# Two output tiles and a raw weight buffer trade pools in a hybrid RWKV/pool/expert layer

## The chip, the cores and the metric

The kernel runs on one core of a Trainium2 chip. The metric is device microseconds of one execution. A profiled execution leaves a trace of every instruction on the five engines (PE for matmuls, DVE, ACT, POOL, and SP, which here only issues transfers) and of every transfer; times in it count from the first instruction.

## The reference, cut to what matters

One layer is computed for 1056 positions (1024 of a prompt, 32 of samples). Behind the mixing part stands the expert part, with 16384 single-neuron experts of which each position uses 8 x 16:

```python
q = (xb @ wq).reshape(PEER_BLOCK, PEER_HEADS, 2, PEER_DK_HALF)
s1 = jnp.einsum('thc,nc->thn', q[:, :, 0], sub_keys[0])
s2 = jnp.einsum('thc,nc->thn', q[:, :, 1], sub_keys[1])
v1, i1 = lax.top_k(s1, PEER_TOPK)
v2, i2 = lax.top_k(s2, PEER_TOPK)
...
ue = jnp.take(u_tab, expert, axis=0)
act = jax.nn.gelu(jnp.einsum('thkd,td->thk', ue, xb).astype(jnp.float32), approximate=False) * gate
ve = jnp.take(v_tab, expert, axis=0)
return jnp.einsum('thk,thkd->td', act.astype(xb.dtype), ve)
```

A gated embedding and a last norm follow.

## The kernel before, in words

The positions are worked in four groups (`GROUPS`). For each group `phase_c` makes the output projection and the norm, then the queries from 16 blocks of `wq`, and writes scores to DRAM (`sc_d`). `top` and `select` then pick experts on DVE. For the first 672 positions (`ND`) the experts are computed densely: the gates are spread into a full table `g_d` in DRAM, by one-hot tiles `ab` that DVE builds (L905 to L907), matmuls over them (L913), a copy into a staging tile `gst` on ACT (L914) and a write of 2 MB per 32 positions (L916). These matmuls are called gate matmuls below. The other 384 positions gather their experts one by one on POOL (L1229).

The dense part takes all 128 expert blocks of `u` (u blocks, `ublock`) and then of `v` (v blocks, `vblock`). Each block is a raw weight tile of 512 KB loaded by SP (L1094), split into two parts for an exact product by `esplit` (`ehi` by ACT at L1096, `elo` by DVE at L1098, or by POOL through `PTT`, L127), and 48 matmuls (L1120) of 128 by 336 over the stored input `XH`, `XL`, or over gated activations `wh`, `wl`. A u block ends in a Gelu on ACT (L1126) that writes an activation tile. The first eight u blocks (`NPRE`, numbered 0 to 7 here) write into the tiles `OT0` to `OT7`, which later hold the sums of the v blocks; the others write into `wt`. `ugate` multiplies an activation tile with its gates, loaded back from `g_d` into `gq` (L1174, L1177), and splits it into `wh` and `wl` (L1181). The first v block needs the gated activations of u blocks 0 to 7.

The part around the change is step 4 of the loop over groups. There the gate table of the third group's last 128 positions is still being made (`t_stream`), `phase_c` runs for the fourth group, and `upre` traces u blocks 0 to 7 between its pieces. The last six of the fourth group's `wq` blocks go through `esplit` as well (`C3E`), the others load ready-made halves `whi` and `wlo` of 256 KB each (L644, L645, three buffers each).

Memory is given out by pools, and a tile that reuses room waits until its last user is done. Pool `dr` is opened before step 4 in room that is free by then. Pool `late` is opened inside step 4 after `gstack.close()`, in the room of pool `gp`, which holds `gst`, `ab` and the one-hot sources. `gp` stays in use until the last gate matmul. In the kernel before, `dr` holds `XH`, `XL`, three raw buffers `eraw`, two each of `ehi` and `elo`, and `OT0` to `OT5`; `late` holds `OT6`, `OT7` and three `wt`.

Buffers of one name are handed out in the order in which the program traces their users. A scheduler then writes each engine's instructions in a fixed order, from priorities in that order and its own estimate of when room and inputs are there. On the chip each engine and the SP queue go through their list in that order.

Of the kernel before, what the change touches and what calls it, by code (L numbers as in the profile page):

```python
# [10 lines left out]
F32 = mybir.dt.float32  # L11
# [9 lines left out]
KB = D // 128  # L21
# [21 lines left out]
ND = GB - GA  # L43
# [20 lines left out]
def body(ctx, tc, io):  # L64
# [557 lines left out]
    def wblock(gi, b):  # L622
        if b >= C3E and gi == NG - 1:
            hi, lo = esplit(io["wq"][b - KB], PTT)
            return [(t[0], t[1]) for t in zip(*[(x[:, :HK], x[:, HK:]) for x in (hi, lo)])]
        out = []
        for i in range(1 if b < KB else 2):
            ks = slice(i * HK, (i + 1) * HK)
            hi = ws.tile([128, HK, 128], F32R, name="whi", bufs=3)
            lo = ws.tile([128, HK, 128], F32R, name="wlo", bufs=3)  # L630
            if gi == 0:
                if b < 4:
                    raw = tk.tile([128, HK, 128], F32, name="wraw", tag="oh", bufs=2)
                else:
                    if b % 4 == 0 and i == 0:
                        wraws[0] = gp.tile([128, EB, TC], F32, name="gst", bufs=2)
                    raw = v3(wraws[0][:, 16 * (b % 4 if b < KB else 2 * (b % 4) + i):][:, :16].rearrange("p a b -> p (a b)"), 128)
                nc.sync.dma_start(raw, (io["w_out"][b] if b < KB else io["wq"][b - KB])[:, ks, :])
                ACT(hi, raw, AF.Copy)
                TT(lo, raw, hi.bitcast(F32), op=ALU.subtract)  # L640
                nc.sync.dma_start(wc_d[b, :, 0, ks, :], hi.bitcast(F32))
                nc.sync.dma_start(wc_d[b, :, 1, ks, :], lo.bitcast(F32))
            else:
                nc.sync.dma_start(hi.bitcast(F32), wc_d[b, :, 0, ks, :])  # L644
                nc.sync.dma_start(lo.bitcast(F32), wc_d[b, :, 1, ks, :])  # L645
            out.append((hi, lo))
        return out
# [438 lines left out]
    DP = ((0, NH), (NH, NH))  # L1086
    U = {}

    def PD():
        return dps.tile([128, 2, 512], F32, name="pd")  # L1090

    def esplit(src, sub=TT):
        raw = dr.tile([128, KB, 128], F32, name="eraw", bufs=3)
        nc.sync.dma_start(raw, src)  # L1094
        hi = dr.tile([128, KB, 128], F32R, name="ehi", bufs=2)
        ACT(hi, raw, AF.Copy)  # L1096
        lo = dr.tile([128, KB, 128], F32R, name="elo", bufs=2)
        sub(lo, raw, hi.bitcast(F32), op=ALU.subtract)  # L1098
        return hi, lo

    OT = {}

    def otile(db):
        if db not in OT:
            OT[db] = (dr if db < KB - 2 else late).tile([128, ND], F32, name=f"OT{db}")
        return OT[db]

    def wt_tile():
# [13 lines left out]
    def ublock(b, sub=TT):  # L1122
        ps = PD()
        emm(ps, esplit(io["uT"][b], sub), xs, DP)
        U[b] = otile(b) if b < NPRE else wt_tile()
        ACT(halves(U[b]), ps[:, :, :NH], AF.Gelu)  # L1126
# [7 lines left out]
    for step in range(1, NG + 1):  # L1134
# [8 lines left out]
        if step == NG:  # L1143
# [3 lines left out]
            late = ctx.enter_context(tc.tile_pool(name="late", bufs=1, side="right", reuse_waits="tile"))  # L1147
# [3 lines left out]
        if step == NG - 1:  # L1151
            nc.sync.dma_start(io["wkv_p"], S[-1])
            pbx.close()
            dr = ctx.enter_context(tc.tile_pool(name="dr", bufs=1, side="right", reuse_waits="tile"))
# [29 lines left out]
    def vblock(g, db):  # L1184
        w = esplit(io["vP"][g, db])
        ps = PD()
        emm(ps, w, [Ws[b] for b in range(g * VG, (g + 1) * VG)], DP)
        if g:
            TT(halves(OT[db]), ps[:, :, :NH], halves(OT[db]), op=ALU.add)  # L1189
        else:  # L1190
            ACT(halves(OT[db]), ps[:, :, :NH], AF.Copy)
        if g == EB // VG // 2:
            ht = wt_tile()
            nc.sync.dma_start(ht, hT_d[:, db, GA:GB])
            TT(OT[db], OT[db], ht, op=ALU.add)
# [88 lines left out]
    class Tail:  # L1284
# [10 lines left out]
        def gate(self, db, w, pl, mul):  # L1295
            ps = PD()
            emm(ps, w, self.xs, self.parts)
            sg = self.tmp()
            for a, (s, k) in enumerate(self.parts):
                TT(sg[:, s:s + k], ps[:, a, :k], self.r[:, s:s + k], op=ALU.mult)  # L1300
            ACT(sg, sg, AF.Sigmoid)
            if db == KB - 1:
                ACT(small()[:, 0:1], eps_t, AF.Sqrt)
            mul(sg, sg, pl[:, self.o:self.o + self.n], op=ALU.mult)
            l = TT(self.src[db], self.src[db], sg, op=ALU.add).ins
            if db < KB - 1:
                square(self.acc, self.src, db, self.tmp())
            else:
                self.more = [self.tmp()]
                ACT(self.more[0], self.src[db], AF.Square)  # L1310
            return l
# [137 lines left out]
def program(arrays, extra=()):  # L1449
    nc = bacc.Bacc("TRN2", target_bir_lowering=False, num_devices=1)  # L1450
    io = {k: nc.dram_tensor(k, v.shape, mybir.dt.from_np(v.dtype), kind="ExternalInput").ap()
          for k, v in arrays.items()}
    for k, s in list(OUTS.items()) + list(extra):
        io[k] = nc.dram_tensor(k, s, F32, kind="ExternalOutput").ap()
    with tile.TileContext(nc, schedule_with_timeline_sim=True) as tc, ExitStack() as ctx:
        body(ctx, tc, io)
    return nc
# [15 lines left out]
```

## Time and profile before

| | |
|---|---|
| median of 3 runs | 3257.71 us (3257.33 to 3266.85) |
| the profiled execution | 3253.73 us, its span 3252.0 us |
| PE busy | 3096.8 us, 95% of the span |
| DVE, POOL, ACT busy | 80%, 43%, 34% |
| mean granted TensorE clock | 0.975 of full speed |

A row of an instruction group gives engine, line, operation and tiles, then count and durations. A row of a chain or a timeline gives the start in us, the length in us, and what ran. A row of windows gives, for a stretch of time, the busy us of each engine with the number of its instructions, then the granted clock (1.00 is full), the share of the transfer engines that was busy, and GB/s.

### The profile page before, as it was taken

What the parts mean: (1) busy time and instruction counts of PE and PEld (TensorE: products, weight loads), DVE (VectorE), ACT (ScalarE), POOL (GpSimd) and SP (SyncE); (2) the same over time, 40 slices, a digit from 0 to 9 for tenths busy, and PEclk for the clock granted to TensorE, in tenths of its full rate; (3) what the DMA queues carried; (4) which work ended last, traced back from release to release, by engine and by line L of the source; (5) the groups of instructions that cost most, each with busy time, mean ns of one, the idle gap of its engine ahead of it and who ended that gap; (6) DMA issues with size and microseconds to landing.
All of it is one profiled execution on the core that took longest, in us unless ns stands there. A gap on an engine that the chain in (4) does not pass through costs nothing.

```text
span 3252.0 us, 66214 instructions
## 1 busy us (share of the span) xinstructions
PE 3096.8 (95%) x26807; PEld 2978.2 (92%) x26807; DVE 2586.6 (80%) x5094; ACT 1111.1 (34%) x1710; POOL 1389.1 (43%) x1069
## 2 busy tenths in 40 slices
PE   8998899989989688999999999999999999999998
PEld 7887788878878588999999999999999999999997
DVE  6776345479898995988889888888888888888955
ACT  6442323435645553322122222222212212222343
POOL 5211400020020241156666666656566666666632
PEclk9999899989999799999999999999999999999998
DMA  3326467968877868389999999999999999999834
GB/s 119 113 96 147 131 167 225 301 175 255 248 225 235 275 213 277 115 308 332 331 342 349 317 348 345 321 335 355 326 326 347 332 331 338 342 326 343 316 98 139
DMA packets 436419, 858.93 MB, mean 264 GB/s; under 512 B 109841, under 2 KB 230929, under 8 KB 431633
## 3 DMA queue, kind: packets, MB, share of 16 engines
q1 hardware_dynamic: 324848, 448.82, 42.8%
q0 software_dynamic: 111264, 405.88, 34.5%
q8 instruction: 210, 3.44, 0.4%
q14 instruction: 97, 0.79, 0.1%
HBM read 733.99 MB, written 120.60 MB: 263 GB/s over the span
## 4 chain that ended last, share of the span: by engine, by line
PE 81%; DVE 8%; DMA 7%; ACT 2%; issue 1%; POOL 0%; SPq 0%; DVEq 0%; ACTq 0%; POOLq 0%
PE pd L1120 59%; PE ps L470 6%; PE ps L219 4%; PE ps L655 3%; PE ps L657 2%; PE ps L656 2%; DMA wlo<-wc_d 2%; PE ps L913 1%; DMA whi<-wc_d 1%; PE ps L302 1%; PE ps L743 1%; DVE ab L905 1%; PE ps L1027 1%; DMA scq<-sc_d 1%; DMA hx_d<-x 1%
## 5 line engine op out<-in xcount | busy, mean ns | idle before, releaser
L1229 POOL DMA_INDIRECT row<-u,idx x384 | 548.0, 1427 | 311.1 <-DVE row L1237 126.5
L1096 ACT ACTIVATE ehi<-eraw 128x1024 fp32r<-128x1024 f32 x274 | 290.7, 1061 | 1130.9 <-PE pd L1120 1025.4
L1229 POOL DMA_INDIRECT row<-v,idx x384 | 534.6, 1392 | 316.6 <-DVE po L1246 144.0
L1120 PE MATMUL pd<-XL,ehi 128*128 128x336 f32 x2176 | 515.4, 317 | 0.0
L1120 PE MATMUL pd<-XH,elo 128*128 128x336 f32 x2176 | 514.9, 317 | 0.3 <-DVE elo L1098 0.2
L1120 PE MATMUL pd<-XH,ehi 128*128 128x336 f32 x2176 | 512.2, 316 | 2.1 <-DVE tt L1300 2.1
L1120 PE MATMUL pd<-wl,ehi 128*128 128x336 f32 (+1 forms) x2112 | 502.3, 316 | 1.5 <-DVE wl L1181 1.4
L1120 PE MATMUL pd<-wh,elo 128*128 128x336 f32 (+1 forms) x2112 | 503.3, 317 | 0.4 <-DVE elo L1098 0.4
L1120 PE MATMUL pd<-wh,ehi 128*128 128x336 f32 (+1 forms) x2112 | 503.0, 317 | 0.0
L1246 DVE SCALAR_TENSOR_TENSOR po<-row,act,po 128x1024 f32<-128x1024 f32 x381 | 488.5, 1282 | 6.7
L1237 DVE SCALAR_TENSOR_TENSOR row<-row,xt 128x1024 f32<-128x1024 f32 x384 | 455.5, 1220 | 7.1 <-DMA xt<-xt_d 3.5
L1098 DVE TENSOR_TENSOR elo<-eraw,ehi 128x1024 fp32r<-128x1024 f32 x260 | 319.7, 1229 | 75.8 <-ACT ehi L1096 75.2
L1120 PEld LDWEIGHTS pd<-XH,ehi 128*128 128x128 f32 x2176 | 372.5, 189 | 2.6 <-DVE tt L1300 2.5
L1120 PEld LDWEIGHTS pd<-XH,elo 128*128 128x128 f32 x2176 | 373.6, 188 | 0.9 <-DVE elo L1098 0.5
L1120 PEld LDWEIGHTS pd<-XL,ehi 128*128 128x128 f32 x2176 | 371.6, 188 | 0.0
L1120 PEld LDWEIGHTS pd<-wl,ehi 128*128 128x128 f32 x2112 | 361.9, 188 | 2.4 <-DVE wl L1181 2.3
L1120 PEld LDWEIGHTS pd<-wh,elo 128*128 128x128 f32 x2112 | 361.1, 188 | 0.8 <-DVE elo L1098 0.6
L1120 PEld LDWEIGHTS pd<-wh,ehi 128*128 128x128 f32 x2112 | 361.7, 188 | 0.1
L655 PE MATMUL ps<-hi,whi 128*128 128x256 f32 (+1 forms) x592 | 186.8, 317 | 27.6 <-DMA whi<-wc_d 17.2
L1189 DVE TENSOR_TENSOR OT<-pd,OT 128x672 f32<-128x672 f32 x120 | 102.9, 858 | 137.8 <-PE pd L1120 137.2
L914 ACT ACTIVATE gst<-ps 128x512 f32<-128x512 f32 x168 | 170.4, 1105 | 71.7 <-PE ps L913 64.5
L657 PE MATMUL ps<-hi,wlo 128*128 128x256 f32 (+1 forms) x592 | 183.2, 310 | 6.6 <-DMA wlo<-wc_d 6.1
(441 smaller groups left out, 5023.9 us busy)
## 6 DMA issues: line engine op xcount, KB each, us to landing
eraw<-uT SPq DMA_DIRECT2D x128, 512.0 KB, 6.4
eraw<-vP SPq DMA_DIRECT2D x128, 512.0 KB, 6.6
g_d<-gst SPq DMA_DIRECT2D x21, 2048.0 KB, 9.6
gq<-g_d SPq DMA_DIRECT2D x32, 1344.0 KB, 10.2
whi<-wc_d SPq DMA_DIRECT2D x108, 256.0 KB, 4.5
wlo<-wc_d SPq DMA_DIRECT2D x108, 256.0 KB, 4.9
fdc<-fd SPq DMA_DIRECT2D x16, 896.0 KB, 8.4
wc_d<-whi SPq DMA_DIRECT2D x40, 256.0 KB, 4.3
```

The lines of the kernel that those rows point to most:

```text
L219: mm(ps[:, :XW], s[:, k, :], x[:, k, a:b], start=first, stop=last)
L470: mm(o[hs], l[hs], r[hs], start=start, stop=stop)
L655: mm(ps[:, :n], whi[:, kk, :], xhi[:, k, :n], start=k == 0, stop=False)
L657: l = mm(ps[:, :n], wlo[:, kk, :], xhi[:, k, :n], start=False, stop=k == K - 1)
L914: ACT(st[:, :, t2 + q:t2 + q + 4].rearrange("p e t -> p t e"), v3(ps, 128), AF.Copy, scale=1.0 / GS)
L1096: ACT(hi, raw, AF.Copy)
L1098: sub(lo, raw, hi.bitcast(F32), op=ALU.subtract)
L1120: mm(ps[:, a, :n], w_[:, k, :], x_[:, s:s + n], start=first, stop=last)
L1189: TT(halves(OT[db]), ps[:, :, :NH], halves(OT[db]), op=ALU.add)
L1229: nc.gpsimd.indirect_dma_start(out=r[:m], out_offset=None, in_=io[tab], in_offset=bass.IndirectOffsetOnAxis(ap=idx[:m, hh, k:k + 1], axis=0))
L1237: STT(r[:m], r[:m], 1.0, xt[:m], op0=ALU.mult, op1=ALU.mult, accum_out=pre[:m, k:k + 1])
L1246: STT(po[:m], r[:m], act[:m, k:k + 1], po[:m], op0=ALU.mult, op1=ALU.add)
```

## The change

`OT6` and `OT7` move from `late` to `dr`. In exchange the raw buffers `eraw` of `dr` go from three to two, and every third call of `esplit` takes its raw tile from a new single buffer in `late`. `late` is already set when `esplit` is first called, so calls 3, 6, 9 and so on use it. In the order of tracing these are u block 2, u block 5, one `wq` block, u block 7, and then every third block to the end.

```diff
+    late, raws = None, [0]
...
     def esplit(src, sub=TT):
-        raw = dr.tile([128, KB, 128], F32, name="eraw", bufs=3)
+        raws[0] += 1
+        third = raws[0] % 3 == 0 and late is not None
+        raw = late.tile([128, KB, 128], F32, name="eraw3") if third else dr.tile([128, KB, 128], F32, name="eraw", bufs=2)
         nc.sync.dma_start(raw, src)
...
     def otile(db):
         if db not in OT:
-            OT[db] = (dr if db < KB - 2 else late).tile([128, ND], F32, name=f"OT{db}")
+            OT[db] = dr.tile([128, ND], F32, name=f"OT{db}")
         return OT[db]
```

No instruction is added or removed; the lists are rewritten. Behind the change all line numbers from the dense part on are four higher (L1094 becomes L1098, L1120 becomes L1124).

The SP queue before, where the raw tiles of the first u blocks are loaded (`eraw_15119`, `15242`, `15365`, `15576`, `15752` are those of u blocks 0 to 4; `whi`, `wlo` are weight halves for `phase_c`):

```order
L686 DMA y_15076<-y_d_64 128x4x256
L1094 DMA eraw_15119<-uT 128x1024
L1094 DMA eraw_15242<-uT 128x1024
L1094 DMA eraw_15365<-uT 128x1024
L762 DMA scq_16419<-sc_d_68 128x512
L916 DMA g_d_72<-gst_14090 128x32x128
L1094 DMA eraw_15576<-uT 128x1024
L644 DMA whi_15219<-wc_d_70 128x512
L645 DMA wlo_15220<-wc_d_70 128x512
L1094 DMA eraw_15752<-uT 128x1024
```

The SP queue now, at the end of the fourth group's weight loads; `gst_14971` is the staging tile of the last gate matmuls:

```order
L645 DMA wlo_16023<-wc_d_70 128x512
L762 DMA scq_18243<-sc_d_68 128x512
L916 DMA g_d_72<-gst_14971 128x32x128
L1098 DMA eraw3_15365<-uT 128x1024
L1178 DMA gq_16649<-g_d_72 128x2688
L1178 DMA gq_16671<-g_d_72 128x2688
L1098 DMA eraw3_15911<-uT 128x1024
L1098 DMA eraw_16052<-wq 128x1024
L1098 DMA eraw_16085<-uT 128x1024
```

The raw load of u block 2 (`15365`) moved from the third place of the loads to behind the last write of the gate table; those of u blocks 5 and 6 (`15911`, `16085`) and of the first `wq` block (`16052`) follow it. The loads of u blocks 0, 1, 3 and 4 stand early in both lists.

PE before, at the start of u block 2 (`pd_15364`), between a projection block of `phase_c` (`ps_15324`) and gate matmuls (`ab_14335`):

```order
L656 MATMUL ps_15324<-lo_15088,whi_15320 128x256
L657 MATMUL ps_15324<-hi_15087,wlo_15321 128x256
L1120 MATMUL pd_15364<-XH_14394,ehi_15367 128x336 x2
L1120 MATMUL pd_15364<-XL_14395,ehi_15367 128x336 x2
L1120 MATMUL pd_15364<-XH_14394,elo_15369 128x336 x2
L1120 MATMUL pd_15364<-XH_14394,ehi_15367 128x336 x2
L1120 MATMUL pd_15364<-XL_14395,ehi_15367 128x336 x2
L1120 MATMUL pd_15364<-XH_14394,elo_15369 128x336 x2
L1120 MATMUL pd_15364<-XH_14394,ehi_15367 128x336 x2
L913 LDWEIGHTS ab_14335
L913 MATMUL ps_14339<-ab_14335 128x128
```

PE now, at the start of the same u block; `ps_16026` is the last `wq` block with ready-made halves, and the last gate matmuls stand 22 matmuls ahead of `pd_15364`:

```order
L655 MATMUL ps_16026<-hi_15448,whi_16022 128x256
L656 MATMUL ps_16026<-lo_15449,whi_16022 128x256
L657 MATMUL ps_16026<-hi_15448,wlo_16023 128x256
L1124 MATMUL pd_15364<-XH_14394,ehi_15367 128x336 x2
L1124 MATMUL pd_15364<-XL_14395,ehi_15367 128x336 x2
L1124 MATMUL pd_15575<-XH_14394,ehi_15578 128x336 x2
L1124 MATMUL pd_15575<-XL_14395,ehi_15578 128x336 x2
L1124 MATMUL pd_15364<-XH_14394,elo_15369 128x336 x2
L1124 MATMUL pd_15364<-XH_14394,ehi_15367 128x336 x2
```

U block 2 and with it u blocks 3 to 6 (`pd_15575`, `15751`, `15910`, `16084`), which before stood in pieces between the gate matmuls and the projections, now stand in one row behind the last gate matmul. U blocks 0 and 1 stay where they were. Behind the six split `wq` blocks and u blocks 7 and 8, from the first v block on, the lists of all engines run as before, but for the places of a few matmuls at the very end.

## The prediction

> **What bounds the kernel now.** I read the page first, then a table of windows through step 4 and one of the dense stretch, then the chain of waits, the SP queue and the waits of DVE around the last gate matmul.
>
> ```profile
> PE 3096.8 (95%) x26807; PEld 2978.2 (92%) x26807; DVE 2586.6 (80%) x5094; ACT 1111.1 (34%) x1710; POOL 1389.1 (43%) x1069
> ```
> ```profile
> 2400.00:3100.00 700.00, 700.00 (x4563) 699.97 (x4562) 610.27 (x728) 170.99 (x204) 440.47 (x312) 1.00 0.92 330
> ```
> ```profile
> L1126 ACT ACTIVATE OT<-pd x8: 712/734/748, 1124.1 to 1288.4; 128x672 f32<-128x672 f32 x8
> ...
> L1120 PE MATMUL pd<-wh,ehi x52: 311/316/322, 1303.4 to 1329.5; 128*128 128x336 f32 x52
> ```
>
> In the dense stretch PE never stops: 700 us in 700, so 0.1534 us per matmul and 7.36 us per block of 48. Nothing can be won or lost there by buffers. The first v block starts at 1303.4. What counts is when that happens; all behind it follows in the same order. The eight u blocks that must precede it end between 1124.1 and 1288.4, inside step 4:
>
> ```profile
> 1080.00:1100.00 20.00, 8.54 (x70) 6.75 (x68) 20.00 (x95) 8.23 (x11) 3.16 (x8) 0.50 1.07 377
> 1100.00:1120.00 20.00, 15.33 (x114) 14.00 (x112) 20.00 (x76) 11.59 (x16) 10.18 (x6) 0.77 0.88 298
> 1120.00:1140.00 20.00, 17.89 (x152) 16.73 (x150) 20.00 (x66) 13.23 (x20) 5.95 (x5) 1.00 0.65 175
> 1140.00:1160.00 20.00, 19.59 (x153) 19.12 (x153) 19.36 (x80) 9.43 (x14) 10.40 (x6) 1.00 0.85 280
> 1160.00:1180.00 20.00, 16.89 (x129) 15.68 (x128) 20.00 (x44) 12.97 (x20) 12.46 (x10) 1.00 0.46 134
> 1180.00:1200.00 20.00, 17.49 (x159) 16.33 (x157) 20.00 (x100) 11.43 (x17) 5.37 (x9) 0.91 0.70 205
> 1200.00:1220.00 20.00, 17.04 (x145) 16.44 (x145) 16.58 (x55) 11.94 (x18) 5.22 (x1) 0.91 0.77 241
> 1220.00:1240.00 20.00, 17.90 (x146) 16.64 (x146) 15.41 (x39) 8.28 (x12) 0.99 (x1) 0.91 0.82 252
> 1240.00:1260.00 20.00, 14.44 (x114) 13.41 (x113) 7.66 (x19) 7.74 (x10) 2.14 (x1) 0.74 0.84 246
> ```
>
> From 1120 to 1200 DVE (the third busy figure) works 79.4 us of 80: it picks experts and builds one-hot tiles, and it sets the pace. PE is nearly full as well, but with filler: from 1120 to 1260 its busy times add to 121.2 us of 140, and u blocks 2 to 6 are 5 x 7.36 = 36.8 us of that. So 18.8 us stand idle now; without the filler it would be over 55.
>
> From 1200 to the last gate matmul DVE has gaps, and the chain of waits runs through weight halves:
>
> ```profile
> 1235.99 10.88 DMA wlo<-wc_d
> 1246.92 0.58 PE ps L657
> ...
> 1253.23 0.94 PE ps L913 x16
> 1254.17 1.18 PE ps L743 x10
> ...
> 1255.77 10.88 DMA g_d<-gst
> ```
> ```profile
> 1188.82 0.38 SPq L644 DMA_DIRECT2D whi<-wc_d  x1
> ...
> 1190.86 0.37 SPq L916 DMA_DIRECT2D g_d<-gst  x1
> 1191.33 6.31 SPq L644 DMA_DIRECT2D whi<-wc_d  x1
> ...
> 1253.15 0.32 SPq L644 DMA_DIRECT2D whi<-wc_d  x1
> ```
> ```profile
> whi<-wc_d SPq DMA_DIRECT2D x16, 256.0 KB, 4.5
> wlo<-wc_d SPq DMA_DIRECT2D x16, 256.0 KB, 5.4
> ```
>
> A load issued right behind a 2 MB gate write is held at issue for 6.31 us and lands 10.88 us after its issue began, against a median of 5.4. The last gate matmul ends at 1253.23 + 0.94 = 1254.2, so today 1303.4 - 1254.2 = 49.2 us lie between it and the first v block.
>
> **The change, part by part.** *Gelu of u blocks 6 and 7 into a tile that is open earlier.* The rows of PE's waits after 1303 hold one of 1.4 us that has to do with the first activations:
>
> ```profile
> PE pd L1120 <- DVE wl L1181: 1.4, 2, 1.1
> ```
>
> More than 1.4 us cannot be won by handing activations over earlier, and I count it as won, since in the new order six split `wq` blocks and u blocks 7 and 8 give DVE time: -1.4.
>
> *The third raw buffer.* In the dense stretch there are three raw buffers as before: 0. In step 4 the new list of SP puts the raw load of u block 2 behind the last gate write, because its room is that of `ab`. Since split tiles are handed out in order, u blocks 3 to 6 wait with it. Two terms follow.
>
> *First term: the stretch up to the last gate matmul gets shorter.* PE loses 36.8 us of filler there. But DVE and the weight queue held the pace, so only what they lose counts. DVE loses contention: beside each `elo` subtraction on POOL one DVE instruction is stretched.
>
> ```profile
> 1179.56 2.81 POOL L127 TENSOR_TENSOR elo<-eraw,ehi 128x1024 fp32r<-128x1024 f32 x1
> ```
> ```profile
> 1123.80 2.49 DVE L907 TENSOR_TENSOR ab<-ab,e 128x1024 f16<-128x1024 f16 x1
> ...
> 1180.07 2.85 DVE L907 TENSOR_TENSOR ab<-ab,e 128x1024 f16<-128x1024 f16 x1
> ...
> 1183.70 0.68 DVE L907 TENSOR_TENSOR ab<-ab,e 128x1024 f16<-128x1024 f16 x1
> ...
> 1240.39 2.30 DVE L907 TENSOR_TENSOR ab<-ab,e 128x1024 f16<-128x1024 f16 x1
> ```
>
> There are seven such stretched instructions of L906 and L907 from 1123.80 to 1240.39, 10.3 us together over their usual 0.68, and 7.5 us of it up to 1183. All seven subtractions move behind the last gate matmul.
>
> The Trainium skill ("SBUF — State Buffer", section "Who interferes with whom") says that a DVE instruction with two inputs in SBUF and a GpSimd instruction that reads SBUF lock each other out for the whole instruction. By that the seven subtractions (an estimate from their durations of 2.4 to 5.2 us in this trace) could have cost DVE up to 24 us, 14 more than its stretched rows show; then the first term could be larger and the forecast up to 14 us lower, but the rows show the loss itself, so they decide.
>
> DVE also has 12 instructions of L855, L856 and L860 (selection for the gathered positions) that the new order puts behind its last gate tile, and it now waits 8.6 us:
>
> ```profile
> 1217.70 1.29 DVE L855 TENSOR_TENSOR oh<-cF,CF 128x512 f32<-128x512 f32 x2
> ```
> ```profile
> DVE V L765 <- DMA scq<-sc_d: 5.2, 3, 4.6
> DVE ab L905 <- PE ps L913: 3.4, 1, 3.4
> ```
>
> 12 x 0.64 = 7.7. If DVE alone ruled, the last gate matmul could come 10.3 + 7.7 + 8.6 = 26.6 us earlier; that is one end. The other end is 0: the weight queue is what it was. Between them I count the queue. From 1188.82 to 1253.15, 15 halves are issued in 64.3 us. Three gate writes in between hold the queue 6.3 us each, 19 us; the rest is 3.0 us per half. With PE free of filler a buffer cycle is a landing of 5.4 and 12 matmuls of 0.12, 6.8 us for three halves, or 2.3 each: 15 x 0.7 = 11 us sooner. The queue starts about 6 us sooner, most of DVE's 7.5. Against this, a less busy PE runs at a lower clock, which costs these matmuls some 2 us (first two windows: 0.50 and 0.77 at 8.5 and 15.3 us of 20). I take -15.
>
> *Second term: what lies behind the last gate matmul gets longer.* Now 49.2 us. In the new order PE ends the last `wq` halves and then waits for the raw tile of u block 2:
>
> - 1254.2 to the issue of the gate write at 1255.77: 1.6.
> - The raw load behind that 2 MB. Nearest row: the load issued at 1235.99, just behind a gate write, landed after 10.88. With 0.7 for the issue before it and 0.8 for 512 KB in place of 256: 12.4.
> - The split, from the rows below: 1.06 on ACT and 2.37 to 2.67 on POOL, 3.6 together.
>
> ```profile
> L1096 ACT ACTIVATE ehi<-eraw x274: 1039/1061/1096, 1103.1 to 3221.0; 128x1024 fp32r<-128x1024 f32 x137
> ...
> L127 POOL TENSOR_TENSOR elo<-eraw,ehi x14: 2366/2672/5221, 1106.9 to 1288.5; 128x1024 fp32r<-128x1024 f32 x14
> ```
>
> That is 17.6 us until PE runs freely (8 matmuls are done in the wait for POOL). Then come u blocks 2 to 8, 7 x 48 - 8 = 328 matmuls x 0.1534 = 50.3; six split `wq` blocks, 144 x 0.12 = 17.3; 16 key matmuls x 0.118 = 1.9 (1.18 for ten, in the chain above); short waits of 0.7 for the split of a `wq` block, whose 24 matmuls of 2.9 us do not cover 3.6, some 2 in all; and 3 for PE's clock after the wait:
>
> ```profile
> 1107.81 0.41 PE L657 MATMUL ps<-hi,wlo 128*128 128x256 f32 x1
> 1108.02 0.41 PE L655 MATMUL ps<-hi,whi 128*128 128x256 f32 x1
> ...
> 1122.23 0.29 PE L657 MATMUL ps<-hi,wlo 128*128 128x256 f32 x1
> 1122.35 0.28 PE L655 MATMUL ps<-hi,whi 128*128 128x256 f32 x1
> ```
>
> Starts 0.21 us apart at 1108, after the sparse stretch, and 0.12 at 1122: half speed for some 6 us costs 3. The Trainium skill ("TensorE: Matmul & The Clock Gate", section "What's actually happening") says that the clock falls to half after an idle window of about 3.4 us and returns after about 3.4 us of work; by that the loss is 1.7, an estimate, and the sum 1.3 lower.
>
> Together 17.6 + 50.3 + 17.3 + 1.9 + 2 + 3 = 92.1, against 49.2: +42.9.
>
> *Sum.* +42.9 - 15 - 1.4 = +26.5 us. Against the profiled execution's 3253.7 that gives 3280.2; its median of the runs stands 4.0 higher at 3257.7, so I forecast 3284.
>
> **The rivals.** *The stretch does not shorten.* The last gate matmul stays at 1254.2, because gate writes and weight loads share one queue and keep its pace. For it: the landing of 10.88 in the chain. Against: DVE sheds 10 us. Then +41.5: 3299.
>
> *DVE rules and the raw tile comes soon.* The last gate matmul comes 26.6 us earlier, not 15, and the raw load lands as after a plain issue, some 6 us earlier. Then 26.5 - 11.6 - 6 = +9: 3267. Against: each of the gate writes seen holds its follower.
>
> *Faster: PE was the limit.* If the gate matmuls and projections wait in PE's list behind u blocks, taking out 36.8 us there and 10.3 on DVE pulls the last gate matmul forward by 47 us: 42.9 - 47 - 1.4 = -5.5, 3252. It decides once the last gate matmul ends before 1254.2 - 41.5, about 1213. For it: PE works 17 to 19.6 us of 20. Against: DVE is full until 1200 and waits for PE 3.4 us in all.
>
> *It only does what it says.* The output tiles open earlier, the raw loads come no later in effect, because PE finds the same gaps for its u blocks elsewhere. Then 0 to -1.4: 3257. Against: the new PE list has no u block between the gate matmuls after block 1, and PE does not leave its list.
>
> **How the numbers follow.** A difference below 0.3%, 9.8 us, can hardly be told from none here. I give the forecast 60% (with its own ends at first terms of -24 and -4, 3275 to 3295), no shortening 15%, the early raw tile 15%, faster 4%, no effect 6%. Slower by over 0.3% takes the forecast, no shortening and four fifths of the early raw tile: 87%. Same: 9%. Faster: 4%. The range from 3266 to 3300 takes in all but the last two and the edges.
>
> **What would show it.** In the profile of the changed kernel the Gelus of u blocks 2 to 6 should all lie behind the last gate matmul, which should end near 1239; PE should then stand idle about 11 us, released by a raw load; the first v block should start near 1331; windows from 1120 to 1230 should show PE at 12 to 14 us of 20. The second term is wrong if that wait is missing. The whole is wrong if the last gate matmul ends before 1213, or if PE is not full in the dense stretch.

## The result and the profile after

The changed kernel takes 3281.22 us (median of 8 runs, 3274.41 to 3289.36), the kernel before 3264.88 us beside it (8 runs, 3257.33 to 3271.37). The ratio is 1.0060, with a 95% interval from 1.0043 to 1.0077: slower by about 19.6 us (the two medians themselves are 16.3 us apart). One of the executions behind the experiments below, of the kernel with the order edge, ran in a slower state (3796.83 us at a mean clock of 0.745, the other five at 0.970 to 0.973) and is left out of its figures. The profiled execution took 3276.93 us, its span 3275.2 us at a mean clock of 0.971. That is 23.2 us over the span of before, but the two executions were already 4.5 us apart at the first gate write of the stretch (1106.44 and 1101.92, below). Up to there every engine has run the same number of instructions in both (12923 matmuls); of the change only the missing early load of u block 2 lies ahead of that point. In the other kernels below the same write comes anywhere from 1103.54 to 1116.10, so these 4.5 us are most likely not of the change, and 18.7 us remain for it.

The first line of the page reads as before: PE has 6.3 us more of work time for the same 26807 matmuls.

```profile
PE 3103.1 (95%) x26807; PEld 2981.8 (91%) x26807; DVE 2582.7 (79%) x5094; ACT 1110.5 (34%) x1709; POOL 1378.0 (42%) x1069
```

The chain of waits around the last gate matmul (start, length, what ran):

```profile
1223.82 10.77 DMA whi<-wc_d
...
1235.42 1.73 PE ps L913 x16
...
1238.98 10.07 DMA eraw<-uT
...
1249.08 1.06 ACT ehi L1100
...
1250.18 31.34 PE pd L1124 x192
```

The last gate matmul ends at 1237.15. Then the raw weight tile of u block 2 is waited for, its split by ACT, and the u blocks run in one row. The waits of PE from there to the first v block, and the SP queue at that place:

```profile
PE pd L1124 <- ACT ehi L1100: 9.2, 1, 9.2
```
```profile
1238.51 0.37 SPq L916 DMA_DIRECT2D g_d<-gst  x1
1238.98 5.42 SPq L1098 DMA_DIRECT2D eraw<-uT  x1
```

The wait is put down to ACT, which itself waited for the load: 9.2 us of idle PE that the kernel before did not have. The first v block starts here (timeline of PE):

```profile
1326.17 0.47 PE L1124 MATMUL pd<-wh,ehi 128*128 128x336 f32 x2
```

Behind it PE is as full as before:

```profile
1330.00:3100.00 1770.00, 1767.97 (x11504) 1766.84 (x11503) 1549.28 (x2215) 436.33 (x525) 1084.14 (x783) 1.00 0.90 325
```

So in these two executions the time was lost between the first gate write of the stretch and the first v block. Two windows cover that stretch, cut at the last gate write. Columns: length, then busy time and number of instructions of PE, PEld, DVE, ACT and POOL, then the clock. Before:

```profile
1101.92:1255.77 153.85, 131.75 (x1060) 123.95 (x1059) 137.09 (x463) 83.41 (x116) 52.71 (x36) 0.91 0.74 226
1255.77:1303.36 47.59, 43.13 (x321) 41.53 (x321) 25.62 (x77) 18.73 (x29) 12.07 (x5) 1.00 0.86 296
```

After:

```profile
1106.44:1238.51 132.07, 101.61 (x853) 92.20 (x853) 119.52 (x443) 74.45 (x106) 26.50 (x29) 0.85 0.79 240
1238.51:1326.17 87.66, 77.36 (x529) 75.95 (x528) 38.23 (x98) 27.12 (x37) 28.72 (x12) 0.93 0.56 192
```

Read these as an account. The number of matmuls is the same (1381 and 1382, some shared by neighbouring rows), so the length is PE's busy time plus PE's idle time. The part ahead of the last gate write became 21.8 us shorter, the part behind it 40.1 us longer: +18.3. Of these, 14.2 us are idle time (26.6 before, 40.8 now) and 4.1 us are busy time: the same matmuls took longer, and the granted clock was lower (0.85 against 0.91 ahead of the last write, 0.93 against 1.00 behind it).

### The profile page after: what moved, and what is told of

Read it like the earlier page. It is cut to its first block, busy times and chain, and to the rows that moved or that the text cites. A ratio compares the mean times of both kernels' runs of the same rounds, so it can differ in the third digit from the quotient of the medians.

```text
span 3275.2 us, 66204 instructions
## 1 busy us (share of the span) xinstructions
PE 3103.1 (95%) x26807; PEld 2981.8 (91%) x26807; DVE 2582.7 (79%) x5094; ACT 1110.5 (34%) x1709; POOL 1378.0 (42%) x1069
## 4 chain that ended last, share of the span: by engine, by line
PE 82%; DVE 7%; DMA 6%; ACT 2%; issue 1%; POOL 1%; SPq 0%; DVEq 0%; ACTq 0%; POOLq 0%
PE pd L1124 60%; PE ps L470 6%; PE ps L219 4%; PE ps L655 3%; PE ps L657 2%; PE ps L656 2%; PE ps L913 2%; DMA wlo<-wc_d 1%; PE ps L302 1%; DMA whi<-wc_d 1%; DVE ab L905 1%; PE ps L743 1%; DMA scq<-sc_d 1%; PE ps L1027 1%; DMA sc_d<-scs 1%
## 5 line engine op out<-in xcount | busy, mean ns | idle before, releaser
L1124 PE MATMUL pd<-XH,ehi 128*128 128x336 f32 x2176 | 510.8, 316 | 11.2 <-ACT ehi L1100 9.2
L1124 PE MATMUL pd<-XL,ehi 128*128 128x336 f32 x2176 | 513.5, 317 | 0.0
L1124 PE MATMUL pd<-XH,elo 128*128 128x336 f32 x2176 | 512.6, 317 | 0.1
L1124 PE MATMUL pd<-wl,ehi 128*128 128x336 f32 (+1 forms) x2112 | 503.0, 317 | 1.7 <-DVE wl L1185 1.5
L1124 PE MATMUL pd<-wh,elo 128*128 128x336 f32 (+1 forms) x2112 | 504.0, 317 | 0.4 <-DVE elo L1102 0.4
L1124 PE MATMUL pd<-wh,ehi 128*128 128x336 f32 (+1 forms) x2112 | 503.5, 317 | 0.0
L1124 PEld LDWEIGHTS pd<-XH,ehi 128*128 128x128 f32 x2176 | 372.0, 189 | 11.9 <-ACT ehi L1100 9.4
L1102 DVE TENSOR_TENSOR elo<-eraw,ehi 128x1024 fp32r<-128x1024 f32 x260 | 319.7, 1230 | 78.7 <-ACT ehi L1100 77.9
L1124 PEld LDWEIGHTS pd<-XH,elo 128*128 128x128 f32 x2176 | 372.4, 188 | 1.0 <-POOL elo L127 0.9
L1124 PEld LDWEIGHTS pd<-XL,ehi 128*128 128x128 f32 x2176 | 370.9, 188 | 0.0
L1124 PEld LDWEIGHTS pd<-wl,ehi 128*128 128x128 f32 x2112 | 362.4, 188 | 2.6 <-DVE wl L1185 2.5
L1124 PEld LDWEIGHTS pd<-wh,elo 128*128 128x128 f32 x2112 | 361.7, 188 | 0.8 <-DVE elo L1102 0.7
L1124 PEld LDWEIGHTS pd<-wh,ehi 128*128 128x128 f32 x2112 | 362.2, 188 | 0.1
```

Source lines behind the costliest of these rows:

```text
L1124: mm(ps[:, a, :n], w_[:, k, :], x_[:, s:s + n], start=first, stop=last)
```

## The experiments

All ratios are to the kernel before, run on the same chip in the same session, with 95% intervals. The stretch of the last two fences serves as the measure in each. "To the last write" is from the first gate write to the last, "behind" from there to the first v block, "idle" the length of both less PE's busy time in them. Each is worked out from two SP rows, one PE row and two rows of windows of that kernel's trace.

| kernel | to the last write | behind | PE idle | ratio |
|---|---|---|---|---|
| before | 153.9 | 47.6 | 26.6 | 1 |
| the change | 132.1 | 87.7 | 40.8 | 1.0060 |
| third buffer late, output tiles as before | 132.7 | 88.0 | 39.5 | 1.0075 |
| late buffer from the sixth split on | 144.5 | 71.1 | 37.2 | 1.0051 |
| late buffer from the fifteenth split on | 147.8 | 58.7 | 32.7 | 1.0018 |
| two raw buffers, no third | 146.4 | 58.8 | 31.0 | 1.0106 |
| u blocks behind, pools of before | 147.1 | 72.6 | 39.3 | 1.0062 |
| the same, small subtraction | 139.8 | 71.2 | 33.8 | 1.0040 |
| before, small subtraction | 142.3 | 56.7 | 24.2 | 0.9990 |
| the change, small subtraction | 130.8 | 86.5 | 39.1 | 1.0049 |
| late loads by ACT | 133.9 | 87.8 | 40.6 | 1.0078 |
| before, u blocks traced sooner | 157.9 | 52.6 | 36.2 | 1.0052 |
| fifteenth split and sooner | 147.7 | 61.0 | 34.9 | 1.0019 |

Except with two raw buffers, the stretch grows by the same amount as the whole kernel, to within 8 us. Each stretch is that of one execution, so differences of a few us between them may be noise.

**Which half of the exchange costs.** The change with the output tiles put back where they were:

```diff
-            OT[db] = dr.tile([128, ND], F32, name=f"OT{db}")
+            OT[db] = (dr if db < KB - 2 else late).tile([128, ND], F32, name=f"OT{db}")
```

> The kernel before with one half of the change: every third raw tile comes from the pool late, but OT6 and OT7 stay in late. If the third raw tile, waiting for the room of the one-hot tiles, holds back u blocks 2 to 6 (the theory of the held blocks), this half alone costs what the whole change costs, ratio 1.005 to 1.007 to the kernel before (+16 to +23 us), with the last gate matmul near 1233 on the old time axis and the first v block 89 us behind it. If the moved output tiles are the cause, it costs nothing: 0.999 to 1.001.

3280.44 us, 1.0075 (1.0061 to 1.0089), a little above the 1.005 to 1.007 expected. The late raw buffer, with only two left in the early pool, carries the loss alone. Where the output tiles lie makes no difference that can be told: the intervals overlap, and the stretch is the same to within 1.1 us. PE's wait for the late raw tile is here too:

```profile
PE pd L1124 <- ACT ehi L1100: 9.0, 1, 9.0
```

**The same exchange without the hold.** The third buffer is taken from the late pool only from the fifteenth split on, when its room is free:

```diff
-        third = raws[0] % 3 == 0 and late is not None
+        third = raws[0] % 3 == 0 and raws[0] > 14
```

> The whole change, but the late buffer is used only from the fifteenth split on, so all splits of step 4 share two raw buffers in dr and none waits for late. Theory of the held blocks: u blocks 2 to 6 go back between the gate matmuls, the loss goes, 0.998 to 1.002. Rival, two raw buffers in dr are too few for step 4 whatever the third does: most of the loss stays, 1.003 to 1.007.

3264.40 us, 1.0018 (1.0006 to 1.0030). The theory of the held blocks fits: most of the loss is gone; some 6 us stay. The u blocks stand between the gate matmuls again, and no wait for a raw tile is left behind the last one. The part behind is 11 us longer than in the kernel before (352 matmuls in place of 321, and 5.4 us more of idle time), the part ahead 6 us shorter. Where these 6 us in the total come from is taken up again below: the kernel with two raw buffers has them as well.

**Fewer blocks held.** The late buffer from the sixth split on (`raws[0] > 5`), so that u blocks 2, 3 and 4 stay where they were and blocks 5 and 6 are held:

> The whole change, but the late buffer is first used by the sixth split, which is u block 5, so only u blocks 5 and 6 are held behind the last gate matmul, not 2 to 6. Theory of the held blocks: the wait of PE for a raw tile (9 us) stays, the work moved behind is 14.7 us in place of 36.8, so the first v block comes some 69 us behind the last gate matmul (89 in the changed kernel, 49 before), and the stretch before it shortens by less; 1.002 to 1.005. Rival, the loss is the wait of PE for the raw tile alone: the loss is as large as with the whole change, 1.005 to 1.007.

3272.55 us, 1.0051 (1.0034 to 1.0067), between the last two: two held blocks cost 16.6 us where five cost 19.6. The loss is not in proportion to the number of held blocks. Holding two is already told apart from holding none by the intervals, and is not told apart from holding five. The ratio lies between the ranges of the theory and its rival, so the trace has to decide between them. The wait for a raw tile that I had expected to stay is not there. PE waits about as long for a weight half instead, which the queue issues only at 1266.89, behind the 2 MB write (1258.97):

```profile
1272.93 0.58 PE L655 MATMUL ps<-hi,whi 128*128 128x256 f32 x1 [8.96 <-DMA whi<-wc_d]
```

So the loss does not need the wait for the raw tile. Whether it needs a wait of that length behind the last write is asked by the next kernel.

**The order without the late room.** The kernel before, all three raw buffers in the early pool, and an edge that keeps the matmuls of u blocks 2 to 6 behind the last gate matmul:

```diff
-        emm(ps, esplit(io["uT"][b], sub), xs, DP)
+        w = esplit(io["uT"][b], sub)
+        with tc.issue_after(lastg[0]) if 2 <= b <= 6 else nullcontext():
+            emm(ps, w, xs, DP)
```

> The pools of the kernel before, with an ordering edge that puts the matmuls of u blocks 2 to 6 behind the last gate matmul. Their raw tiles are loaded early, so no wait for a raw tile is left, only the order. Theory: the first v block 70 to 75 us behind the last gate matmul, that one 15 to 20 us earlier than before, so +4 to +9 us, 1.001 to 1.003; the other 12 us of the loss is the wait for the raw tile. Rival, the wait is all of it and the order is free: 0.999 to 1.000. Rival, the order is all of it: 1.005 to 1.007.

3275.05 us, 1.0062 (1.0045 to 1.0080): the same as the change, to within the intervals. I had expected less, since the raw tiles are there in time, and they are: behind the last write 72.6 us pass in place of 87.7, and PE is idle for 1.1 us of them. But ahead of it the gain is 6.8 us in place of 21.8. So the place of the matmuls is enough for a loss of this size, without any wait for a raw load. That the totals come out alike is in part chance: against this kernel the late room adds 15.1 us behind the last write, the wait of 9.2 us among them, and takes 15.0 us off the part ahead. The waits of PE ahead of the last write, here and then in the change, are the place to look for the reason of the latter:

```profile
PE ps L655 <- DMA whi<-wc_d: 12.5, 4, 5.7
PE ps L914 <- ACT gst L915: 5.5, 11, 1.7
PE ps L914 <- DVE ab L908: 4.7, 3, 3.1
PE ps L709 <- POOL sa L127: 3.8, 1, 3.8
```
```profile
PE ps L655 <- DMA whi<-wc_d: 8.5, 3, 4.3
PE ps L913 <- DVE ab L907: 6.3, 6, 2.0
PE ps L913 <- DVE ab L906: 5.9, 2, 4.9
```

Three differences offer themselves: the splits of u blocks 2 and 3 still ran on POOL between the gates, the weight loads met the gate writes at other places, and 28 more matmuls stand ahead of the last write (881 against 853; an estimate from 0.12 us for each matmul of a projection gives 3 us). The next three kernels take the first apart.

**POOL's subtractions.** In each kernel POOL's subtraction in the splits ahead of the dense stretch is cut to one eighth: the `lo` part of the first of eight slices is computed and used for all, seven of eight are left out.

```diff
-        sub(lo, raw, hi.bitcast(F32), op=ALU.subtract)
+        if sub is PTT:
+            PTT(lo[:, 0], raw[:, 0], hi[:, 0].bitcast(F32), op=ALU.subtract)
+            lo = lo[:, 0:1, :].to_broadcast([128, KB, 128])
+        else:
+            sub(lo, raw, hi.bitcast(F32), op=ALU.subtract)
```

In the kernel before:

> The kernel before, with GpSimd's subtraction in the u and wq splits ahead of the dense stage cut to one eighth (the lo part of the first of eight k slices is computed and used for all eight; the other seven are left out, so that many lo values are wrong). Theory of the first term (GpSimd's subtractions stretch VectorE's L906 and L907 by about 10 us in sum, and VectorE sets the pace of the gates): last gate matmul 6 to 10 us nearer to the y split than the 151.8 us of before, total lower by 4 to 9 us, ratio 0.997 to 0.999. Rival (VectorE has slack elsewhere, and the first term came from TensorE's and the queue's work that moved): within 2 us, ratio 0.9995 to 1.0005.

In the kernel with the order edge:

> The pools of before with u blocks 2 to 6 held behind the last gate matmul by an order edge, and GpSimd's subtraction in the u and wq splits ahead of the dense stage cut to one eighth (seven of eight lo slices left out). It asks why the order alone gained 7 us ahead of the last gate where the change gained 22. Theory (the splits of u blocks 2 and 3 still ran between the gates there and stretched VectorE): from the first to the last gate write 132 to 140 us in place of 147, total 6 to 12 us below that of the order alone, ratio to before 1.002 to 1.0045. Rival (what differs is where the projections and weight loads came to stand, not the splits): 143 to 148 us, ratio 1.005 to 1.0065.

In the changed kernel:

> The whole change, with GpSimd's subtraction in the u and wq splits ahead of the dense stage cut to one eighth (seven of eight lo slices left out). Control for the same cut in the kernel before, which brought the last gate write 11.5 us closer to the first. Theory (in the change the subtractions of u blocks 2 to 6 and of wq no longer meet VectorE's gate work, only those of u blocks 0 and 1 do): from the first to the last gate write 128 to 132 us against 132.1, total 0 to 4 us below the change, ratio to before 1.005 to 1.006. Rival (the cut shortens something other than VectorE's gate work): the last gate write 8 to 12 us closer here too.

| small subtraction in | last gate write comes nearer by | ratio, against the same kernel without |
|---|---|---|
| before | 11.5 us | 0.9990 (0.9978 to 1.0003), 1 |
| the order edge | 7.3 us | 1.0040 (1.0027 to 1.0054), 1.0062 |
| the change | 1.3 us | 1.0049 (1.0032 to 1.0066), 1.0060 |

The subtractions that ran beside DVE's gate work did cost the gates about 11 us in the kernel before, and in the change that cost is gone already; the kernels with the order edge and with the change came out as their theories had it, to within the intervals. DVE shows where the 11 us come from. In the kernel before with the small subtraction its 463 instructions ahead of the last write, as many as without, take 124.21 us in place of 137.09:

```profile
1105.91:1248.24 142.33, 126.30 (x1034) 120.28 (x1034) 124.21 (x463) 83.03 (x114) 32.49 (x36) 0.91 0.77 240
```

That bears out the part of the first term that is contention. It also explains a part of the gap between the order edge and the change: 147.1 and 132.1 are 15.0 us apart, 139.8 and 130.8 still 9.0. That rest stays open; the other differences were not taken apart.

The kernel before shows something else. Its last gate write comes 11.5 us nearer, but the first v block only 2.4 us (47.6 + 153.9 against 56.7 + 142.3), and the total falls by 3.3 us where 4 to 9 were expected, which the interval does not tell from nothing. More matmuls were left for behind the last write (349 in place of 321), and PE waited longer for weight halves there; with the small subtraction, and before:

```profile
PE ps L655 <- DMA whi<-wc_d: 5.7, 1, 5.7
```
```profile
PE ps L655 <- DMA whi<-wc_d: 1.7, 1, 1.7
```

The gates had been finished earlier, and that was not worth much by itself.

**What the raw load waits for.** The change, with the loads into the late buffer issued by ACT:

```diff
-        nc.sync.dma_start(raw, src)
+        (nc.scalar if third else nc.sync).dma_start(raw, src)
```

> The whole change, with the raw loads into the late buffer issued by ScalarE in place of SyncE; TensorE's order is that of the change. In the changed kernel the first of them was issued right behind the 2 MB gate write on SyncE, held there 5.42 us, landed 10.07 us after its issue, and TensorE waited 9.2 us. Theory (the price is the room: the load can't start before the last gate matmul; how long it takes is a matter of the queue behind the write): the wait falls from 9.2 to 3 to 5 us, total 3 to 6 us below the change, ratio to before 1.004 to 1.005. Rival (the 2 MB write fills all DMA engines, whoever issues the next load): wait 8 to 10 us, ratio 1.006 as the change.

3285.13 us, 1.0078 (1.0062 to 1.0095): no gain. The wait is 8.8 us. The issue is no longer held, yet the tile comes only 1.1 us sooner behind the write:

```profile
1251.75 0.38 ACTq L1098 DMA_DIRECT2D eraw<-uT  x1
1259.44 2.00 ACT L1100 ACTIVATE ehi<-eraw 128x1024 fp32r<-128x1024 f32 x2 [7.32 <-DMA eraw<-uT]
```

The split starts 9.5 us after the gate write's issue (1249.96), against 10.6 us in the change. So the held issue on SP is not what keeps the tile back. That it is the 2 MB transfer itself is most likely, but not shown: ACT's own list put the issue 1.8 us behind the write, from there to the split pass 7.7 us in place of 10.1, and no run put the load ahead of the write.

**What the third raw buffer is worth.** The output tiles in the early pool, two raw buffers and no third:

```diff
-        raw = dr.tile([128, KB, 128], F32, name="eraw", bufs=3)
+        raw = dr.tile([128, KB, 128], F32, name="eraw", bufs=2)
...
-            OT[db] = (dr if db < KB - 2 else late).tile([128, ND], F32, name=f"OT{db}")
+            OT[db] = dr.tile([128, ND], F32, name=f"OT{db}")
```

> The output tiles of the seventh and eighth block in the early pool and only two raw buffers, no third one anywhere: the exchange without its late half. The u blocks stay between the gate matmuls, except that u block 7 still runs behind the wq projection. My theory (what costs is the third buffer's late room, which holds five u blocks back): no such hold here, so near the kernel with the late buffer from the fifteenth split on, 3264 us, ratio 1.001 to 1.003; the few us above before are then the price of the second raw buffer's depth in steps 3 and 4, and the third late buffer from the fifteenth split on is worth under 3 us. Rival (a third raw buffer is worth much in the dense stage, where splits follow each other every 7 us): over 3275 us, ratio above 1.005.

3291.08 us, 1.0106 (1.0091 to 1.0121). My theory had 3264 and fell; the rival held. The stretch is that of the kernel with the late buffer from the fifteenth split on, to within 1.4 us. The difference shows in the dense stretch, where the waits of PE, which were none, now hold a row:

```profile
PE pd L1120 <- DVE elo L1098: 18.6, 12, 2.4
```

So the third raw buffer saves 18.6 us of waits in the dense stretch, of the 26.7 us between the two medians (of different sessions, in which the kernel before differed by 1.0 us); the rest was not taken apart. In the change it still does that, from the late pool. And since the stretch ahead is 3.8 us longer here than in the kernel before (205.2 against 201.4) and 5.1 us longer with the buffer from the fifteenth split on, the 6 us that remained there most likely belong to having only two raw buffers during step 4. That wasn't run with the output tiles in their old place.

**Blocks sooner.** The stream of the eight u blocks is traced at weight 12 in place of 8, so that u block 7 comes between the gate matmuls, in the kernel before and in the one with the late buffer from the fifteenth split on:

```diff
-            streams = [streams[1], (NPRE, upre())]
+            streams = [streams[1], (12, upre())]
```

> The kernel before, with the stream of the eight u blocks merged at weight 12 in place of 8, so that their splits are traced sooner: u block 7 comes between gate matmuls ahead of the wq splits, and none is left behind the last gate matmul. Theory (PE work that stands between gate matmuls fills waits, and the same work behind the last gate matmul costs its full 10 us per block): the distance from the last gate matmul to the first v block falls by some 10 us, the last gate matmul comes up to 5 us later, total lower by 3 to 10 us, ratio 0.997 to 0.999. Rival (the stretch ahead of the last gate is as full as it can be, and each further block stretches it by its own length): within 2 us.

> The whole change, with the late raw buffer used only from the fifteenth split on and the u blocks' stream at weight 12: output tiles of the seventh and eighth block open early, no u block waits for the late room, and u block 7 runs between gate matmuls. Theory: the sum of the last two effects, so 3264 less 3 to 10 us: 3254 to 3261 us, ratio 0.999 to 1.001 to before, and not better than the kernel before with weight 12. Rival (the earlier output tiles pay only once all eight u blocks fit ahead of the last gate matmul): below 3250 us, ratio under 0.998.

The first gave 3274.51 us, 1.0052 (1.0034 to 1.0069), the second 3264.01 us, 1.0019 (1.0007 to 1.0032). Both theories fell, and so did the rivals: in the kernel before, one more block between the gates lengthens both parts (157.9 and 52.6), and idle time rises by 9.6 us; in the other it changes nothing. The block did come ahead of the last gate matmul (382 matmuls of u blocks there in place of 333), but projections fell back behind it in exchange (81 of their matmuls behind it in place of 48), and they wait for weight halves there. The profiled execution of the first shows 9 of its 15.7 us in the stretch; the rest isn't in that trace. No kernel of this study is clearly faster than the kernel before.

## Why the prediction was right, point by point

**The mechanism.** The prediction held that the late room of u block 2's raw tile puts u blocks 2 to 6 behind the last gate matmul, and that this shortens the stretch ahead of it by less than it lengthens the one behind. The waits and the two window rows show it, and so do the Gelus of u blocks 1, 2 and 6:

```profile
1139.95 0.73 ACT L1130 ACTIVATE OT<-pd 128x672 f32<-128x672 f32 x1 [1.52 <-PE pd L1124]
1262.21 0.73 ACT L1130 ACTIVATE OT<-pd 128x672 f32<-128x672 f32 x1
...
1292.68 0.71 ACT L1130 ACTIVATE OT<-pd 128x672 f32<-128x672 f32 x1
```

The two halves of the exchange run apart show that it is the late buffer and not the output tiles. The loss is 19.6 us where 26.5 were forecast. That the absolute figure came nearer (3284 against 3281.22) is luck: beside the change the kernel before ran 7 us longer than in the three runs that the forecast stood on.

**First term, -15.** Measured from the first gate write, the last gate matmul ends 21.5 us sooner (130.7 us after it against 152.3), inside the term's ends of 0 and -26.6 but 6.5 us beyond the value taken. Of its parts the contention with POOL is borne out: 10.3 us were read from stretched rows, 11.5 us came out when the subtractions were cut. The part for moved instructions came nearly whole: of the 24 instructions of L855, L856 and L860 ahead of the last gate write, 10 moved behind it (12 were counted), and their time there fell from 15.6 to 9.3 us, by 6.3 where 7.7 were read. With both, DVE's busy time ahead of the last write fell by 17.6 us (137.09 to 119.52). The part for its waits did not come: DVE still waits in the change (6.1 us for gate matmuls, 4.0 us for a copy on ACT):

```profile
DVE ab L905 <- PE ps L913: 6.1, 3, 4.9
DVE oh L855 <- ACT cF L832: 4.0, 1, 4.0
```

What made the term too small is what it counted for the weight queue. The load issued at 1188.82, where the count began (86.9 us after the first gate write), is the ninth `whi` of the stretch. In the change the ninth comes 66.3 us after the first gate write, 20.6 us sooner where the term had 6. The fifteen pairs of halves from there (the prediction calls them 15 halves) then take 51.1 us in place of 64.3, 13.2 us less where it had 11. (The three holds in the 64.3 us were 6.31, 5.38 and 5.72 us, 17.4 and not 19.) The norm ahead of these loads also ends 13.4 us sooner, measured from the first gate write, and not for contention alone: up to the norm DVE works without a gap to speak of in both, but with 188 instructions in place of 234, as the new list puts more of the picking behind the norm. The rows of the norm, before and now:

```profile
1169.35 5.14 DVE L714 SCALAR_TENSOR_TENSOR h<-h,vecs,rstd 128x256 f32<-128x256 f32 x8
```
```profile
1160.04 5.60 DVE L714 SCALAR_TENSOR_TENSOR h<-h,vecs,rstd 128x256 f32<-128x256 f32 x8
```

The prediction had nothing for that, and no run took it apart.

The Trainium skill ("SBUF — State Buffer", section "Who interferes with whom") would have allowed, as an estimate, for up to 24 us of contention, by a lock for the whole instruction; cutting seven eighths gave 11.5, so here the stretched rows were the better measure.

**Second term, +42.9.** From the last gate matmul to the first v block 1326.17 - 1237.15 = 89.0 us pass, against 92.1 forecast: +39.8. The raw tile's load landed 10.5 us after the write's issue, not 12.4, and half clock after the wait cost less than the 3 us counted. (The 6.31 us of hold and the 10.88 us to landing that the prediction read together are of two loads; the one that landed after 10.88 was held 5.72.) The timeline of PE shows it, two matmuls to a row:

```profile
1250.18 0.93 PE L1124 MATMUL pd<-XH,ehi 128*128 128x336 f32 x2 [9.16 <-ACT ehi L1100]
...
1252.03 0.76 PE L1124 MATMUL pd<-XL,ehi 128*128 128x336 f32 x2
...
1253.38 0.49 PE L1124 MATMUL pd<-XH,ehi 128*128 128x336 f32 x2
1253.71 0.47 PE L1124 MATMUL pd<-XL,ehi 128*128 128x336 f32 x2
```

Rows start 0.56 to 0.73 us apart until 1253.38 and 0.31 to 0.33 apart from there on, and 192 matmuls took 31.34 us where 192 x 0.1534 is 29.5: a loss of 1.9 us, the last wait for POOL among it. The Trainium skill ("TensorE: Matmul & The Clock Gate", section "What's actually happening") gave 1.7 for this, an estimate, with about 3.4 us of work until the clock is back; the 3.2 us seen here agree, and the 1.7 was nearer than my 3 from the sparse stretch.

**Third term, -1.4.** It did not come. The wait that I counted as won is there as before:

```profile
PE pd L1124 <- DVE wl L1185: 1.5, 2, 1.3
```

Together -21.5 + 39.8 + 0 = +18.3. The step that was mis-sized most is the first term, by 6.5 us, and in it the start of the weight queue.

**The rivals.** "The stretch does not shorten" falls with the 21.5 us. "PE was the limit" would need a last gate matmul before 1213; it came at 1237. "It only does what it says" falls with the order of PE, which held. "DVE rules and the raw tile comes soon" has its first half nearly right and its second wrong: the load is late whoever issues it.

**What would show it.** The wait behind the last gate matmul (9.2 us for about 11), its end (1237 for 1239) and the first v block (1326 for 1331) came near what was said, the last two in part by luck: this execution was 4.5 us late at the first gate write already, and counted from there they came 6 and 9 us sooner than said. The windows did not: from 1120 to 1230 PE worked 85.8 us of 110, or 15.6 of 20, not 12 to 14. Only one was half empty:

```profile
1120.00:1140.00 20.00, 19.20 (x166) 17.95 (x164) 20.00 (x75) 12.65 (x19) 2.22 (x3) 1.00 0.64 193
1140.00:1160.00 20.00, 9.90 (x85) 8.08 (x82) 20.00 (x64) 8.82 (x14) 2.93 (x4) 0.86 0.87 261
1160.00:1180.00 20.00, 16.59 (x115) 13.89 (x116) 19.27 (x63) 11.20 (x20) 7.49 (x8) 0.71 0.48 168
1180.00:1200.00 20.00, 15.18 (x144) 14.27 (x143) 15.12 (x69) 9.69 (x15) 3.42 (x8) 0.91 0.90 268
```

I had taken away the filler and left the rest of the work spread over the old time, though the term itself said that the stretch gets shorter; and projections at a lower clock keep PE busy for longer.

**"Nothing can be won or lost there by buffers."** This sentence on the dense stretch was wrong as a general one. It held for the change, which keeps three raw buffers; with two, 18.6 us were lost there.

## What to carry to other kernels

Where one engine has the same instructions to run between two fixed points, sum its idle time between them before pricing single waits: work that fills the gaps of a stage which waits for other engines costs less than its own length there, and its full length once it is moved behind that stage. How much less has to be measured: without five blocks of together 36.8 us this stage got 6.8 us shorter in one kernel and 21.8 in another, and one block more in it was not free either. A buffer that takes reused room holds back not only its own user but every later one that takes tiles in order from the same small rings, so ask when the room becomes free before putting an early user in it. And a stage that ends sooner is worth only what its end was holding up: gates that ended 11.5 us earlier brought 2.4 us.

## What the runs showed of the hardware

- A 512 KB load issued behind a 2 MB write was ready late from either engine: from SP, 0.5 us behind and held at issue for 5.42 us, 10.6 us after the write's issue; from ACT, 1.8 us behind and issued in 0.38 us, 9.5 us after it.
- Fewer matmuls in a stretch went with a lower clock for the rest. With 853 in 132.07 us in place of 1060 in 153.85 us ahead of the last gate write the granted clock fell from 0.91 to 0.85, and over the whole stretch the same matmuls took 4.1 us more of busy time.
